# Softmax maximum over the keys: one GpSimd all-reduce in place of transposes, a row maximum and a copy

## The chip, the cores and the metric

The kernel runs on one core of a Trainium2 chip. Its engines are TensorE (PE, with its weight loads PEld), VectorE (DVE), ScalarE (ACT), GpSimd (POOL) and SyncE (SP), each with its own queue of instructions, worked off in order. The metric is the device time of one execution in microseconds, lower is better.

## The reference

One layer of a bidirectional encoder in float32: 2048 tokens of width 1024 with 16 learned meta tokens ahead of them (2064 keys). Four query heads share two key/value heads of width 128, beside them runs a Fourier mixing group, then an output projection and an MLP of width 4096. The part that matters here is the softmax over all keys:

```
s = jnp.einsum('bkgqd,bksd->bkgqs', qb, kt).astype(jnp.float32) * scale
p = jax.nn.softmax(s, axis=-1).astype(vt.dtype)
return jnp.einsum('bkgqs,bksd->bkgqd', p, vt)
```

For each query and head the maximum over all 2064 keys is subtracted ahead of the exponential.

## The kernel before

The program runs in stages: projections of the tokens (to about 310 us), attention (softmaxes from 346 to 985 us), and the MLP with its products in the Strassen manner (to the end). Attention shares its time with other work that is traced between its steps: the Fourier group's transforms, the output projection of the Fourier part (`out_f`, tiles pof, ysq, rs_f, xo) and that of the attention part (`out_a` and `flip`, tiles poa, rs_a, rs_m, h, pmt).

Attention has 16 units, each with 256 queries of two heads (512 columns) against all keys. A unit has 17 steps, one for each block of 128 keys and a last one for the meta tokens (`K = NT + 1`). Scores lie with the keys on the partitions and the 512 query columns in the free dimension:

- `scores(u, i)`: three products give a block of scores in PSUM, ScalarE copies it into an S tile (L780, two blocks to a tile), VectorE keeps the running maximum M over the blocks (L783 for the first, L786, L788, and L775 for the meta tokens). M is one tile with one buffer (`bufs=1`); at the end M[partition, column] is the maximum over the keys that share a partition.
- `stats(u)`: takes M over the 128 partitions and spreads the result to all of them, as the tile mb. `over_keys` (L794, L796) makes four TensorE transposes of 128x128 into the PSUM tile pm_m and a VectorE row maximum mx_m (128x4). `rows_to_cols` (L803) makes four more transposes of broadcast columns into pd_m, and ScalarE copies pd_m to mb (L811).
- `softmax(u, i)`: VectorE subtracts mb from an S tile (L840; L820 for the meta tokens), ScalarE takes the exponential (L841), VectorE sums (L845, L847), TensorE multiplies with V (L849, tile o).
- `finish(u)`: the sums over the keys go through `over_keys` and `rows_to_cols` as well (tiles pm_l, mx_l, pd_l), and the result is scaled and stored.

The PSUM tiles pm_m, pd_m, pm_l, pd_l and pys share one bank ("misc"). The scores run ahead of the softmax by one unit and three steps (`more(n + 1 + K + LEADT)`, LEADT = 3). `stats` of a unit is a generator: its first part is traced a step after that unit's last scores, its second part one step later, and `softmax(u, 0)` follows. The S tiles have 11 buffers, so the scores can't run further ahead.

GpSimd has three kinds of work in attention: the loads of K, q and V from DRAM (L704, L738, L713), the adds of squares ysq (L954) and the powers of -0.5 that give the norms' factors rs_f, rs_a and rs_m (L192, in `rstd_of`, a `tensor_tensor` with `ALU.pow`).

The order of the instructions on each engine is set at build time by the framework's scheduler, from the traced order, priorities and its own costs of the instructions; on the chip each engine then keeps that order and waits on semaphores.

Of the kernel before, what the change touches and what calls it, by code (L numbers as in the profile page):

```python
# [5 lines left out]

# [5 lines left out]
F32 = mybir.dt.float32  # L12
R32 = mybir.dt.float32r
AF = mybir.ActivationFunctionType
ALU = mybir.AluOpType
# [4 lines left out]
P = 128  # L20
# [68 lines left out]
def bc(ap, shape):  # L89
    return ap.broadcast_to(shape)  # L90
# [45 lines left out]
def encoder_block(ctx: ExitStack, tc: tile.TileContext, x, meta, w_in, w_f,  # L136
                  w_out, w_up, w_down, g_fin, g_cols, g_rows, c_id, c_rope, c_dft, c_even, c_odd, c_rem, out):
    nc = tc.nc
# [553 lines left out]
    ap2 = Lines(tc.alloc_tile_pool(name="ap2", bufs=1, side="right", reuse_waits="tile"), small)  # L692

    def misc(name, shape=(P, 512)):
        return app.tile(list(shape), F32, name=name, tag="misc")
# [33 lines left out]
    def attention():  # L729
# [60 lines left out]
        def over_keys(x, name, op):  # L790

            ps = misc("pm_" + name, (P, 4, P))
            for a in range(4):
                nc.tensor.transpose(ps[:, a], x[:, a * P:(a + 1) * P], ident)  # L794
            r = ap2.tile([P, 4], F32, name="mx_" + name, tag="mx", bufs=2)
            nc.vector.tensor_reduce(r, ps, axis=AX.X, op=op)  # L796
            return r

        def rows_to_cols(vec, name):

            ps = misc("pd_" + name, (P, 4, P))
            for a in range(4):
                nc.tensor.transpose(ps[:, a], bc(vec[:, a:a + 1], [P, P]), ident)  # L803
            return ps.rearrange("p a e -> p (a e)")

        def stats(u):
            s = state[u]
            r = over_keys(s["M"], f"m{u}", ALU.max)
            yield
            mb = s["mb"] = ap2.tile([P, 512], F32, name=f"mb_{u}", tag="mb", bufs=2)  # L810
            nc.scalar.copy(mb, rows_to_cols(r, f"m{u}"))  # L811

        def softmax(u, i):

# [76 lines left out]
        def more(upto):  # L891
            while ahead[0] < min(upto, total):
                w, i = divmod(ahead[0], K)
                if i == K // 2 and w < len(units) - 1:
                    start(w + 1)
                scores(w, i)
                loads_next("k", w, i)
                ahead[0] += 1
                if i == NT:
                    later.append(stats(w))  # L900
# [6 lines left out]
        for n in range(total):  # L907
            u, i = divmod(n, K)
# [826 lines left out]
```

## Time and profile before

| what | value |
|---|---|
| median of 3 runs | 2256.49 us (2255.51 to 2256.86) |
| the profiled execution | 2255.64 us, its span 2253.6 us |
| granted TensorE clock | 0.999 |
| busy: PE, DVE, ACT, POOL | 99%, 75%, 52%, 11% of the span |
| maxima over the keys | 16, the first begun at 343.6 us, the last at 956.1 us |

A row of a group reads: line, engine, operation, output<-inputs, shapes, count, then the busy time and the mean of one in ns, then the idle time of the engine ahead of them and what ended it. In a timeline a row begins with the start and the duration in us. "x2" merges two instructions that follow each other. PE's durations overlap, since matmuls are pipelined: the distance between two starts is the price of one.

### The profile page before, as it was taken

Reading aid. Unit: us, or ns where it says so; the run is one execution under the profiler, and the core shown is the slowest. Engines: PE = TensorE matmul, PEld = TensorE weight load, DVE = VectorE, ACT = ScalarE, POOL = GpSimd, SP = SyncE. Lnnn points to the kernel's source line nnn. Section 1 sums busy time; section 2 is a strip of 40 time slices with the busy share of each in tenths; the row PEclk is TensorE's granted clock in tenths of the full one; section 3 lists DMA queues with packets and bytes.
Section 4 is the critical chain, followed back from the end, with each engine's and each line's share of the span. In section 5 each row is a group of like instructions: output and inputs, shape, how many; then the busy total and the mean of one; then the engine's idle time right before and its main releaser. Section 6 shows DMA issues by size and latency. Waiting matters only on the chain.

```text
span 2253.6 us, 28116 instructions
## 1 busy us (share of the span) xinstructions
PE 2233.3 (99%) x10238; PEld 1771.3 (79%) x10238; DVE 1692.9 (75%) x2250; ACT 1178.1 (52%) x1997; POOL 247.8 (11%) x285
## 2 busy tenths in 40 slices
PE   9999999999999999999999999999999999999998
PEld 7898987766667666677888888888888888888887
DVE  6334579999999889788677668788765656796795
ACT  6443356666555566668556563334455545443343
POOL 2212120003322122110000020000110000200000
PEclk9999999999999999999999999999999999999999
DMA  6332253123344434357777576445594444954342
GB/s 205 90 108 70 86 149 90 52 65 130 113 133 131 158 128 133 137 208 256 264 233 241 181 290 227 132 143 167 185 362 169 154 154 152 343 178 159 126 137 84
DMA packets 191786, 367.40 MB, mean 163 GB/s; under 512 B 15760, under 2 KB 74768, under 8 KB 189984
## 3 DMA queue, kind: packets, MB, share of 16 engines
q1 hardware_dynamic: 171040, 310.08, 40.8%
q0 software_dynamic: 20464, 55.27, 7.6%
q8 instruction: 80, 1.31, 0.2%
q14 instruction: 58, 0.48, 0.1%
q10 hardware_dynamic: 144, 0.26, 0.0%
HBM read 236.28 MB, written 129.27 MB: 162 GB/s over the span
## 4 chain that ended last, share of the span: by engine, by line
PE 89%; DVE 5%; ACT 2%; DMA 1%; issue 1%; POOL 1%; SPq 0%; POOLq 0%; ACTq 0%; DVEq 0%
PE o L849 7%; PE ux L82 5%; PE ux L80 5%; PE ux L81 5%; PE dx L82 5%; PE dx L81 5%; PE dx L80 5%; PE dy L82 4%; PE dy L81 4%; PE dy L80 4%; PE uy L82 4%; PE uy L80 4%; PE uy L81 4%; PE s L80 2%; PE s L82 2%; PE s L81 2%
## 5 line engine op out<-in xcount | busy, mean ns | idle before, releaser
L70 ACT CAST ah<-a 128x1024 fp32r<-128x1024 f32 x108 | 113.0, 1050 | 263.2 <-PE dx L81 108.5
L849 PE MATMUL o<-S,vn 128*128 128x512 f32 x512 | 243.6, 596 | 4.2 <-ACT S L841 3.4
L780 ACT COPY S<-s 128x512 f32<-128x512 f32 x256 | 145.0, 584 | 92.4 <-PE s L82 73.1
L82 PE MATMUL dx<-bh,al 128*128 128x512 f32 x496 | 192.5, 388 | 0.0
L81 PE MATMUL dx<-bl,ah 128*128 128x512 f32 x496 | 192.5, 388 | 0.0
L80 PE MATMUL dx<-bh,ah 128*128 128x512 f32 x496 | 192.5, 388 | 0.0
L82 PE MATMUL ux<-bf,wul 128*128 128x512 f32 x448 | 174.2, 389 | 0.7 <-DVE wul L71 0.7
L80 PE MATMUL ux<-bf,wuh 128*128 128x512 f32 x448 | 174.6, 390 | 0.0
L81 PE MATMUL ux<-bf,wuh 128*128 128x512 f32 x448 | 174.3, 389 | 0.0
L840 DVE TENSOR_TENSOR S<-S,mb 128x1024 f32<-128x1024 f32 x128 | 155.1, 1227 | 11.7 <-ACT mb L811 11.6
L841 ACT ACTIVATE S<-S 128x1024 f32<-128x1024 f32 x128 | 135.1, 1062 | 43.0 <-DVE S L840 41.8
L71 DVE TENSOR_TENSOR al<-a,ah 128x1024 fp32r<-128x1024 f32 x108 | 131.2, 1219 | 31.6 <-ACT ah L70 31.3
L849 PEld LDWEIGHTS o<-S,vn 128*128 128x128 f32 x512 | 92.1, 189 | 75.2 <-issue 59.0
L80 PE MATMUL dy<-bh,ah 128*128 128x512 f32 (+1 forms) x388 | 150.5, 388 | 0.0
L81 PE MATMUL dy<-bl,ah 128*128 128x512 f32 (+1 forms) x388 | 150.5, 388 | 0.0
L82 PE MATMUL dy<-bh,al 128*128 128x512 f32 (+1 forms) x388 | 150.5, 388 | 0.0
L80 PE MATMUL s<-q,kt 128*128 128x512 f32 (+1 forms) x272 | 145.3, 534 | 2.3 <-ACT S L780 2.0
L80 PE MATMUL uy<-bf,wuh 128*128 128x512 f32 x320 | 125.0, 391 | 0.3 <-ACT wuh L70 0.3
L82 PE MATMUL uy<-bf,wul 128*128 128x512 f32 x320 | 124.6, 390 | 0.7 <-DVE wul L71 0.7
L81 PE MATMUL uy<-bf,wuh 128*128 128x512 f32 x320 | 124.8, 390 | 0.0
L786 DVE TENSOR_TENSOR M<-M,S 128x1024 f32<-128x1024 f32 x96 | 117.6, 1225 | 8.9 <-ACT S L780 8.0
L1212 ACT ACTIVATE c<-c 128x512 f32<-128x512 f32 x96 | 60.5, 631 | 119.4 <-DVE c L1260 116.6
(323 smaller groups left out, 5708.3 us busy)
## 6 DMA issues: line engine op xcount, KB each, us to landing
a<-s_d SPq DMA_DIRECT2D x84, 512.0 KB, 3.7
R<-in_w_up_dram SPq DMA_DIRECT2D x32, 1024.0 KB, 5.5
s_d<-s SPq DMA_DIRECT2D x128, 256.0 KB, 2.1
s_d<-c SPq DMA_DIRECT2D x96, 256.0 KB, 2.7
d<-in_w_down_dram SPq DMA_DIRECT2D x48, 512.0 KB, 5.2
f_d<-lf SPq DMA_DIRECT2D x56, 256.0 KB, 2.8
bf<-f_d SPq DMA_DIRECT2D x7, 2048.0 KB, 14.3
a<-s_d POOLq DMA_DIRECT2D x24, 512.0 KB, 7.3
```

Of the source, the lines that this page charges most:

```text
L70: self.high = nc.scalar.copy(hi, src)
L71: self.low = nc.vector.tensor_tensor(lo, src, f32v(hi), op=ALU.subtract)
L80: nc.tensor.matmul(out, a[0], b[0], start=first, stop=False, skip_group_check=chain)
L81: nc.tensor.matmul(out, a[0], b[1], start=False, stop=False, skip_group_check=chain)
L82: nc.tensor.matmul(out, a[1], b[0], start=False, stop=last, skip_group_check=chain)
L780: nc.scalar.copy(S[:, i % 2], ps)
L786: nc.vector.tensor_tensor(M, M, S, op=ALU.max)
L840: nc.vector.tensor_tensor(S, S, mb, op=ALU.subtract)
L841: nc.scalar.activation(p, S, AF.Exp, scale=ISQ)
L849: nc.tensor.matmul(s["O"], v[:, 2 * j % 4 + e], p[:, e], start=i + e == 1, stop=False)
L1212: nc.scalar.activation(dst, src, AF.Relu)
```

## The change

`partition_all_reduce` is one GpSimd instruction that reads M (128x512), takes the maximum over the 128 partitions and writes it to all partitions of mb. It stands in place of `over_keys`, `rows_to_cols` and the copy in `stats`. The rest of attention is as it was, the sums' transposes too. The generator still has one yield, now behind the whole work, so mb is complete in its first part.

```diff
+from concourse import bass_isa
...
         def stats(u):
             s = state[u]
-            r = over_keys(s["M"], f"m{u}", ALU.max)
-            yield
             mb = s["mb"] = ap2.tile([P, 512], F32, name=f"mb_{u}", tag="mb", bufs=2)
-            nc.scalar.copy(mb, rows_to_cols(r, f"m{u}"))
+            nc.gpsimd.partition_all_reduce(mb, s["M"], P, bass_isa.ReduceOp.max)
+            yield
```

More of the change, by code (lines that the diff above doesn't have):

```diff
@@ L807, in stats @@
             s = state[u]
-            r = over_keys(s["M"], f"m{u}", ALU.max)
+            mb = s["mb"] = ap2.tile([P, 512], F32, name=f"mb_{u}", tag="mb", bufs=2)
+            nc.gpsimd.partition_all_reduce(mb, s["M"], P, bass_isa.ReduceOp.max)
             yield
-            mb = s["mb"] = ap2.tile([P, 512], F32, name=f"mb_{u}", tag="mb", bufs=2)
-            nc.scalar.copy(mb, rows_to_cols(r, f"m{u}"))
         def softmax(u, i):
```

## The prediction

> **What bounds the kernel now.** I read the page first (busy shares, slices), then the busy times by stage, the groups of instructions, the waits, and last the timelines around one maximum. All rows are of the profile of before.
>
> ```profile
> span 2253.6 us, 28116 instructions
> ...
> PE 2233.3 (99%) x10238; PEld 1771.3 (79%) x10238; DVE 1692.9 (75%) x2250; ACT 1178.1 (52%) x1997; POOL 247.8 (11%) x285
> ```
>
> The shares over the whole span say: TensorE is the bound, GpSimd has nothing to do. But the edit lives in attention alone, between the first maximum (343 us) and the last softmax (985 us), and there the balance is another one. Columns of the next view: stretch, its length, then busy time of each engine.
>
> ```profile
> 343.00:420.00 77.00, 76.63 (x358) 53.79 (x357) 74.26 (x90) 48.77 (x78) 6.49 (x10) 1.00 0.27 74
> 420.00:660.00 240.00, 235.81 (x987) 160.03 (x986) 232.01 (x290) 145.95 (x250) 53.07 (x47) 1.00 0.31 99
> 660.00:985.00 325.00, 322.58 (x1279) 219.95 (x1278) 286.83 (x356) 197.95 (x323) 63.31 (x53) 1.00 0.39 131
> ```
>
> VectorE is idle for 77 - 74.26 = 2.7 us in the first stretch, 8.0 us in the second and 38.2 us in the third. So for the first 317 us two engines, TensorE and VectorE, are both full; only after 660 is VectorE loose. GpSimd is busy 20% of the time. Granted TensorE clock is 1.00 throughout.
>
> **What is removed.** The edit drops these four groups (16 units, each with 4 + 4 transposes, a row maximum and a copy):
>
> ```profile
> L794 PE MATMUL pm_m<-ident,M 128*128 128x128 f32 x64 | 9.9, 277 | 1.0 <-DVE M L775 1.0
> L803 PE MATMUL pd_m<-ident,mx_m 128*128 128x128 f32 x64 | 10.1, 278 | 0.2 <-DVE mx_m L796 0.2
> L796 DVE TENSOR_REDUCE mx_m<-pm_m 128x4 f32<-128x512 f32 x16 | 11.0, 689 | 6.1 <-PE pm_m L794 5.8
> L811 ACT COPY mb<-pd_m 128x512 f32<-128x512 f32 x16 | 9.4, 585 | 16.5 <-PE pd_m L803 16.4
> ```
>
> Matmuls overlap, so TensorE's price is the distance between starts, not the 277 ns:
>
> ```profile
> 656.83 0.60 PE L794 MATMUL pm_m<-ident,M 128*128 128x128 f32 x4
> 657.26 1.02 PE L849 MATMUL o<-S,vn 128*128 128x512 f32 x2
> 658.21 0.65 PE L803 MATMUL pd_m<-ident,mx_m 128*128 128x128 f32 x4
> 658.61 0.48 PE L80 MATMUL s<-q,kt 128*128 128x512 f32 x1
> ```
>
> 657.26 - 656.83 = 0.43 and 658.61 - 658.21 = 0.40: 0.83 us a unit, 16 x 0.83 = 13.3 us of TensorE. VectorE loses 16 x 0.69 = 11.0 us of work, ScalarE 9.4 us (half idle, worth nothing by itself). The one-bank "misc" PSUM tile is also free sooner for the sums' transposes; that removes waits of tenths of a microsecond at most, counted as nothing. The 128 transposes of the sums stay.
>
> **What is added: one all-reduce of 128x512 on GpSimd per unit.** No row shows it. The nearest are GpSimd's two-input adds:
>
> ```profile
> 543.01 0.72 POOL L954 TENSOR_TENSOR ysq<-ysq 128x256 f32<-128x256 f32 x1 [19.60 <-ACT ysq L952]
> 545.23 0.45 POOL L954 TENSOR_TENSOR ysq<-ysq 128x128 f32<-128x128 f32 x1
> 702.68 1.25 POOL L954 TENSOR_TENSOR ysq<-ysq 128x256 f32<-128x256 f32 x2
> ```
>
> From 128 to 256 elements 0.27 us more: 2.1 ns an element and 0.18 us to start; one pass over 512 elements is 1.26 us. That is the floor: the data must at least go once through the engine. The other end is a reduction that takes lanes one by one; with 16 passes it is 0.18 + 16 x 1.08 = 17.5 us. I take four passes (read and fold within a group of partitions, carry across the groups, carry back, write to all partitions): 0.18 + 4 x 1.08 = 4.5 us, an estimate nearer to the floor, because every row of this engine here is a streaming pass.
>
> The Trainium skill (GPSIMD Engine Reference, Cross-partition — where GPSIMD wins) has a reduction along the partitions of [128, 2048] at 247,699 ns, which by a quarter would be an estimate of 61.9 us for our 512; no run so far shows this instruction. By it the sum would gain 16 x (61.9 - 0.7) - 48.9 = 930 us.
>
> **What it does to VectorE.** While GpSimd reads SBUF, VectorE's operations with two SBUF inputs stand still, and the other way round:
>
> ```profile
> 545.95 2.16 DVE L840 TENSOR_TENSOR S<-S,mb 128x1024 f32<-128x1024 f32 x1
> 548.03 1.48 DVE L786 TENSOR_TENSOR M<-M,S 128x1024 f32<-128x1024 f32 x1
> ...
> 546.26 2.16 POOL L954 TENSOR_TENSOR ysq<-ysq 128x256 f32<-128x256 f32 x2
> ...
> L840 DVE TENSOR_TENSOR S<-S,mb 128x1024 f32<-128x1024 f32 x128 | 155.1, 1227 | 11.7 <-ACT mb L811 11.6
> L786 DVE TENSOR_TENSOR M<-M,S 128x1024 f32<-128x1024 f32 x96 | 117.6, 1225 | 8.9 <-ACT S L780 8.0
> ```
>
> These two took (2.16 - 1.23) + (1.48 - 1.23) = 1.18 us longer than their means while GpSimd did 1.25 us of adds (its unhindered time, above). VectorE pays GpSimd's reading nearly one for one. The reverse:
>
> ```profile
> 894.56 6.61 POOL L192 TENSOR_TENSOR rs_m<-ms_m,mhalf 128x1 f32<-128x1 f32 x1 [7.14 <-DVE ms_m L190]
> ...
> 895.52 1.22 DVE L786 TENSOR_TENSOR M<-M,S 128x1024 f32<-128x1024 f32 x1
> ...
> 900.67 0.74 DVE L1057 SCALAR_TENSOR_TENSOR h<-poa,rs_a,h 128x512 f32<-128x512 f32 x1
> ...
> L192 POOL TENSOR_TENSOR rs_m<-ms_m,mhalf x16: 545/1458/6612, 805.7 to 1025.1; 128x1 f32<-128x1 f32 x16
> ```
>
> A power of one column, 0.55 us at its best, took 6.61 us: it came through when VectorE reached an operation fed from PSUM. So the all-reduce first waits for a break in VectorE's chain (this costs no VectorE time, but makes mb late), then holds VectorE for its 4.5 us. Behind the wait stand, on VectorE, the subtraction L840, and L783 of the next unit, since M has one buffer, which is now held until the all-reduce has read it; on GpSimd's queue the K, q and V loads, the squares' adds and the powers.
>
> **The sum by stretch.** Each unit takes from VectorE 4.5 - 0.69 = 3.81 us net. The maxima are 3, 6 and 7 in the three stretches:
>
> ```profile
> L796 DVE TENSOR_REDUCE mx_m<-pm_m x3: 690/691/692, 344.3 to 414.2; 128x4 f32<-128x512 f32 x3
> ...
> L796 DVE TENSOR_REDUCE mx_m<-pm_m 128x4 f32<-128x512 f32 x6 | 4.1, 686 | 0.8 <-PE pm_m L794 0.7
> ...
> L796 DVE TENSOR_REDUCE mx_m<-pm_m 128x4 f32<-128x512 f32 x7 | 4.8, 692 | 4.6 <-PE pm_m L794 4.5
> L840 DVE TENSOR_TENSOR S<-S,mb 128x1024 f32<-128x1024 f32 x64 | 76.6, 1220 | 10.2 <-ACT mb L811 10.2
> ```
>
> First stretch: 3 x 3.81 - 2.7 idle = +8.7 us. Second: 6 x 3.81 - 8.0 = +14.9. In both VectorE becomes the bound and TensorE's savings there are not collected. Third: 7 x 3.81 = 26.7 us fit into 38.2 idle, of which 10.2 + 4.5 = 14.7 us are waits for this very maximum, which the all-reduce replaces; TensorE is the bound and would save 7 x 0.83 = 5.8, of which I credit half, -2.9, since mb comes later. Together +20.7 us. What is late next there is rs_m and rs_a behind the all-reduce.
>
> **The queue of GpSimd.** All-reduces now alternate with tensor_tensor work of another kind, and the engine may have to fetch other code each time:
>
> ```profile
> L954 POOL TENSOR_TENSOR ysq<-ysq x32: 453/960/6802, 503.2 to 736.5; 128x256 f32<-128x256 f32 x16, 128x128 f32<-128x128 f32 x16
> ...
> L796 DVE TENSOR_REDUCE mx_m<-pm_m x11: 676/691/692, 530.2 to 956.4; 128x4 f32<-128x512 f32 x11
> ...
> L192 POOL TENSOR_TENSOR rs_m<-ms_m,mhalf 128x1 f32<-128x1 f32 x10 | 23.9, 2391 | 94.0 <-DVE ms_m L190 94.0
> L192 POOL TENSOR_TENSOR rs_f<-ms_f,mhalf 128x1 f32<-128x1 f32 x16 | 11.3, 707 | 70.6 <-DVE ms_f L190 64.8 <-PE s L82 5.8
> ...
> L713 POOL DMA_DIRECT2D vn<-v_n x20 | 11.5, 579 | 86.4 <-PE o L849 63.2 <-PE pa L567 17.4 <-PE pof L81 5.8
> ...
> vn<-v_n POOLq DMA_DIRECT2D x20, 256.0 KB, 3.1
> ...
> L1069 ACT ACTIVATE h<-h,rs_m 128x1024 f32<-128x1024 f32 x10 | 11.5, 1151 | 16.7 <-POOL rs_m L192 15.5 <-DMA h_d<-h 1.3
> ```
>
> No row shows such a fetch. Bounds: nothing (code resident), or two in each of the 11 units after 503, each at the price of a V load, 0.58 + 3.1 = 3.7 us: 81 us. Some 58 of those tensor_tensors (32 + 16 + 10) fall into 985 - 503 = 482 us, one per 8.3 us, so a fetch of 3.7 us is met by one in 3.7 / 8.3 = 45% of cases: 11 x 0.45 x 3.7 = 18 us, else GpSimd's idle time hides it. ScalarE already waits 15.5 us for rs_m, the rest has slack; I take half, +10 us. If that cover were gone it would be up to the 81.
>
> The Trainium skill (GPSIMD Engine Reference, Instruction dispatch) gives some 6 us for the first call to freshly loaded GpSimd code. By that price this term would be an estimate of 16 us instead of 10, and no row here shows it.
>
> **Total.** 20.7 + 10 = +30.7 on the profiled execution's own 2255.64 us (span 2253.6): 2286.3. That execution lies 0.85 us under the median of the runs, 2256.49; in terms of the median I predict 2287.
>
> **Rivals.**
> 1. *All hidden, faster.* If the all-reduce streams in one pass (1.26 us), it takes 0.57 us net from VectorE, 1.7, 3.4 and 4.0 us in the stretches, all inside the idle time, and the chain from M to the first subtraction is shorter than now:
>
> ```profile
> 342.90 0.69 DVE L775 TENSOR_TENSOR M<-M,S 96x512 f32<-96x512 f32 x1
> ...
> 346.39 1.23 DVE L840 TENSOR_TENSOR S<-S,mb 128x1024 f32<-128x1024 f32 x1 [1.36 <-ACT mb L811]
> ```
>
> 346.39 - 343.59 = 2.8 us today. Then TensorE collects its 13.3: 2256.5 - 13.3 = 2243. It turns at the price where the second stretch has no idle left: 0.69 + 8.0 / 6 = 2.0 us per all-reduce. For it: nothing on the chain is then longer. Against it: a cross-partition result needs more than one pass.
>
> 2. *Lane-serial, far slower.* At 17.5 us VectorE loses 16 x 16.8 - 48.9 = 220 us: with the 10 about 2486. For it: the engine's rows here show no crossing of partitions at all. Against it: a streaming design is what they do show. The Trainium skill's figure above belongs to this case, as its far end.
>
> 3. *Code fetches on the path.* The 4.5 us hold and every fetch is paid: 2256.5 + 20.7 + 81 = 2358. For it: mb, rs_a and rs_m are each awaited. Against it: GpSimd is idle 80% of the time and a fetch needs no data.
>
> 4. *No change.* An all-reduce of about 2 us and some gain on TensorE cancel: 2252 to 2261.
>
> **Chances.** Forecast 0.53 (2262 to 2347; the top is an all-reduce of eight passes, 8.8 us: 16 x 8.1 - 48.9 + 10 = +91), rival 1 0.18, rival 4 0.09, rival 2 0.12, rival 3 0.08. 0.2% is 4.5 us, about what a measurement of this kernel can tell from no change. Faster 0.18, same 0.09, slower 0.73. The range 2243 to 2347 leaves out rival 2, most of rival 3 and a little below rival 1.
>
> **What would show it.** The all-reduce's own row (4.5 us when VectorE is idle, more where it waits for a break); VectorE's L840 and L783 waiting for POOL mb, not ACT mb; two-input VectorE rows above 1.23 us around it; TensorE's idle time in the first two stretches grown by some 31 us (23.6 longer, 9 x 0.83 less work), led by S of L841; rs_m and rs_f later. From 985 us on every stage should keep its length. I am wrong if the all-reduce's row is under 2 us or over 9 us, if VectorE runs on undisturbed beside it, or if the build-time order of the engines puts enough other VectorE work behind each maximum.

## The result, and the profile after

| kernel | median | runs | ratio to before, 95% interval |
|---|---|---|---|
| before | 2256.68 us | 4 | |
| after | 2274.41 us | 4 | 1.0083 [1.0061, 1.0105] |

The change costs 17.7 us (14 to 24 by the interval). The profiled execution took 2274.24 us, with a span of 2272.4 us.

The page of the kernel after, its span and busy times:

```profile
span 2272.4 us, 27939 instructions
...
PE 2233.3 (98%) x10110; PEld 1761.9 (78%) x10110; DVE 1684.1 (74%) x2234; ACT 1173.1 (52%) x1981; POOL 271.1 (12%) x301
```

No engine works longer but GpSimd, and that by 23 us. So the 17.7 us are no added work: the engines wait. (TensorE's busy time has stayed the same with 128 products fewer; a part of that is a lower clock, to which the last section comes back.) The busy times by stage, same stretches as before:

```profile
343.00:420.00 77.00, 74.24 (x324) 49.31 (x322) 69.37 (x82) 45.90 (x73) 14.73 (x13) 1.00 0.25 70
420.00:660.00 240.00, 229.26 (x913) 152.48 (x914) 223.09 (x276) 139.43 (x236) 62.51 (x48) 0.98 0.29 95
660.00:985.00 325.00, 312.17 (x1200) 211.08 (x1198) 272.71 (x340) 189.52 (x310) 68.15 (x64) 0.99 0.40 131
```

TensorE idles 2.8 + 10.7 + 12.8 = 26.3 us of these 642, where it idled 7.0 before. VectorE, which I expected to become the bound, idles more too: 7.6, 16.9 and 52.3 us against 2.7, 8.0 and 38.2. Nothing is full any more; the engines wait for each other.

The stretches are fixed and the work in them slides, so the place of the loss is read from landmarks. The last step of each maximum, with its number and its first and last start: first the rows of before up to the sixth maximum, the ninth and the last, with the first `ux` product of the MLP; then the same rows of after (there the first maximum began just ahead of the window, hence x5 and x8).

```profile
L775 DVE TENSOR_TENSOR M<-M,S x6: 678/686/689, 342.9 to 528.4; 96x512 f32<-96x512 f32 x6
L775 DVE TENSOR_TENSOR M<-M,S x9: 676/685/689, 342.9 to 653.1; 96x512 f32<-96x512 f32 x9
L775 DVE TENSOR_TENSOR M<-M,S x16: 676/686/689, 342.9 to 955.0; 96x512 f32<-96x512 f32 x16
L80 PE MATMUL ux<-bf,wuh x448: 389/389/504, 1034.8 to 1941.4; 128*128 128x512 f32 x150
```

```profile
L776 DVE TENSOR_TENSOR M<-M,S x5: 678/681/683, 375.6 to 530.2; 96x512 f32<-96x512 f32 x5
L776 DVE TENSOR_TENSOR M<-M,S x8: 674/681/941, 375.6 to 664.8; 96x512 f32<-96x512 f32 x8
L776 DVE TENSOR_TENSOR M<-M,S x16: 674/681/941, 342.1 to 973.0; 96x512 f32<-96x512 f32 x16
L81 PE MATMUL ux<-bf,wuh x448: 389/389/497, 1053.6 to 1960.2; 128*128 128x512 f32 x150
```

Up to the sixth maximum after is 1.8 us late (530.2 against 528.4), at the ninth 11.7, at the sixteenth 18.0; the MLP starts 18.8 us later and keeps its length. The first maximum had come 0.8 us earlier than in before, so 2.6 us are lost up to the sixth. Most of the loss begins at about 530 us, when the output projection's adds and powers come onto GpSimd's queue (the first such add of before starts at 503.2). TensorE's products with S in before, between 343 and 985 us, and then the groups of after that answer to those shown of before:

```profile
L849 PE MATMUL o<-S,vn 128*128 128x512 f32 x511 | 243.2, 596 | 4.2 <-ACT S L841 3.4 <-ACT O L855 0.7
```

```profile
L810 POOL PARTITION_ALL_REDUCE mb<-M x16: 1800/1802/4948, 346.8 to 979.1; - x16
...
L840 DVE TENSOR_TENSOR S<-S,mb 128x1024 f32<-128x1024 f32 x128 | 156.9, 1237 | 27.6 <-POOL mb L810 27.6
L849 PE MATMUL o<-S,vn 128*128 128x512 f32 x512 | 248.3, 607 | 12.8 <-ACT S L841 11.3
L810 POOL PARTITION_ALL_REDUCE mb<-M x16 | 35.9, 2242 | 93.4 <-issue 39.5 <-DVE M L776 11.8 <-DVE wol L75 7.9
```

The all-reduce takes 1.80 us, not 4.5. VectorE's subtraction waits 27.6 us for it, where it waited 11.6 for ScalarE's mb, and TensorE waits 11.3 us for the S behind that, where it waited 3.4. And GpSimd itself idles 39.5 us ahead of its all-reduces on "issue", which means: for nothing that the profile shows. One such place, the seventh maximum. GpSimd's timeline:

```profile
573.48 0.56 POOL L193 TENSOR_TENSOR rs_f<-ms_f,mhalf 128x1 f32<-128x1 f32 x1
...
574.58 0.73 POOL L739 DMA_DIRECT2D q<-q_d  x1
582.47 1.80 POOL L810 PARTITION_ALL_REDUCE mb<-M  x1 [7.16 <-issue]
591.57 1.53 POOL L193 TENSOR_TENSOR rs_f<-ms_f,mhalf 128x1 f32<-128x1 f32 x1 [7.30 <-DVE mx_l L797]
```

VectorE's and TensorE's at the same time:

```profile
572.18 0.67 DVE L776 TENSOR_TENSOR M<-M,S 96x512 f32<-96x512 f32 x1
...
584.30 1.23 DVE L840 TENSOR_TENSOR S<-S,mb 128x1024 f32<-128x1024 f32 x1 [5.89 <-POOL mb L810]
585.56 0.68 DVE L825 TENSOR_TENSOR ph<-S,ph 32x512 fp32r<-32x512 f32 x1
...
586.30 0.79 PE L829 MATMUL o<-ph,vm 96*128 96x512 f32 x1 [5.82 <-DVE ph L825]
```

M is complete at 572.85. GpSimd has nothing left to do from 575.31 and still starts only at 582.47; mb comes at 584.27, 11.4 us after M. VectorE stands at L840, and behind it in VectorE's queue stands `ph` of the unit before, for which TensorE waits 5.8 us. Such a gap of 5.8 to 7.9 us stands ahead of 12 of the 16 all-reduces, all those with a `tensor_tensor` as the last computing instruction ahead of them on GpSimd. The other four (the second to the fifth maximum) follow another all-reduce and start 0.1 to 0.2 us after M. A gap of some 7 us stands on the way back, too (584.27 to 591.57). This is what a fetch of other code looks like here: idle time with no named cause, on each change of kind. That the time goes into fetching code is inferred from this pattern; no row names it.

### The profile page after: what moved, and what is told of

Read it like the earlier page. It is cut to its first block, busy times and chain, and to the rows that moved or that the text cites. A ratio compares the mean times of both kernels' runs of the same rounds, so it can differ in the third digit from the quotient of the medians.

```text
span 2272.4 us, 27939 instructions
## 1 busy us (share of the span) xinstructions
PE 2233.3 (98%) x10110; PEld 1761.9 (78%) x10110; DVE 1684.1 (74%) x2234; ACT 1173.1 (52%) x1981; POOL 271.1 (12%) x301
## 4 chain that ended last, share of the span: by engine, by line
PE 87%; DVE 7%; issue 2%; POOL 2%; ACT 1%; DMA 1%; SPq 0%; POOLq 0%; DVEq 0%; ACTq 0%
PE o L849 7%; PE ux L83 5%; PE ux L81 5%; PE ux L82 5%; PE dx L83 5%; PE dx L82 5%; PE dx L81 5%; PE dy L82 4%; PE dy L83 4%; PE dy L81 4%; PE uy L81 4%; PE uy L82 4%; PE uy L83 4%; PE s L81 2%; PE s L83 2%
## 5 line engine op out<-in xcount | busy, mean ns | idle before, releaser
L849 PE MATMUL o<-S,vn 128*128 128x512 f32 x512 | 248.3, 607 | 12.8 <-ACT S L841 11.3
L840 DVE TENSOR_TENSOR S<-S,mb 128x1024 f32<-128x1024 f32 x128 | 156.9, 1237 | 27.6 <-POOL mb L810 27.6
L841 ACT ACTIVATE S<-S 128x1024 f32<-128x1024 f32 x128 | 135.0, 1061 | 76.2 <-DVE S L840 75.8
```

What stands on the lines that cost most here:

```text
L840: nc.vector.tensor_tensor(S, S, mb, op=ALU.subtract)
L841: nc.scalar.activation(p, S, AF.Exp, scale=ISQ)
L849: nc.tensor.matmul(s["O"], v[:, 2 * j % 4 + e], p[:, e], start=i + e == 1, stop=False)
```

## The experiments

The theory after this reading: the hold of VectorE is small, and the 17.7 us come from fetching code on GpSimd at each change between `tensor_tensor` and the all-reduce. The rival: the hold of VectorE by the all-reduce is the cost, the gaps are hidden. A third possibility is the order of the instructions, which the build sets anew for every kernel; the traces show which kernels share it. In what follows a difference is one of medians, each taken against the kernel before in its own job, and the figure behind a time is its ratio to before, with the 95% interval.

**Without `tensor_tensor` on GpSimd in attention.** Both kernels get the same edit: the powers by logarithm and exponential on ScalarE, the squares' adds on VectorE. The first run is the kernel after, the second the kernel before.

```diff
+    nc.scalar.preload_act_table_set("natural_log_exp_and_others")
...
-        nc.gpsimd.tensor_tensor(rs[:rows], ms[:rows], mhalf[:rows, :n], op=ALU.pow)
+        if tag in ("f", "a", "m", "m2"):
+            nc.scalar.activation(rs[:rows], ms[:rows], AF.Ln)
+            nc.scalar.activation(rs[:rows], rs[:rows], AF.Exp, scale=-0.5)
+        else:
+            nc.gpsimd.tensor_tensor(rs[:rows], ms[:rows], mhalf[:rows, :n], op=ALU.pow)
...
-                nc.gpsimd.tensor_tensor(sq[:, :n], sq[:, :n], sq[:, n:2 * n], op=ALU.add)
+                nc.vector.tensor_tensor(sq[:, :n], sq[:, :n], sq[:, n:2 * n], op=ALU.add)
```

> The changed kernel with the all-reduce as the only code of its kind on GpSimd during attention: the powers rs_f, rs_a, rs_m become two ScalarE instructions (logarithm, exponential of -0.5 times it), the adds of ysq go to VectorE. Theory A (GpSimd fetches other code before each all-reduce that follows tensor_tensor work and again after it, some 6 us each, and mb waits for it): the gaps of 5.8 to 7.9 us ahead of the all-reduces from the sixth unit on and the gaps of 7 us behind them go, M to mb is 2 to 4 us in all 16 units, and the kernel is 15 to 30 us faster than the changed one, at or below the kernel before (2240 to 2260). Theory B (the all-reduce holds VectorE: 16 x 1.8 - 11.0 = 18 us): the hold stays, 2268 to 2280. Theory C (the loss lies in the order that the build set): no telling, but near 2274.

> Control: the kernel before with the same move of powers and adds off GpSimd, the transposes kept. All theories: within 6 us of the kernel before (2250 to 2260), since VectorE does the adds in 0.7 us a tile pair where GpSimd held it for 1.2. Theory A: e1 lies 0 to 13 us under this one (TensorE's 13.3 us less work, minus what mb comes later). Theory B: e1 lies about 18 us above it.

Measured: 2253.63 us, 0.9988 [0.9979, 0.9998], for the all-reduce; 2251.10 us, 0.9976 [0.9966, 0.9986], for the transposes. The edit is worth 5.8 us in the kernel before, and 17.7 + 3.3 = 21.0 us in the kernel after. So 15.2 us of the change's 17.7 are there only while `tensor_tensor` and all-reduces alternate; the intervals of the three kernels leave some 6 us either way on that. Without the alternation the all-reduce stands 2.5 us behind the transposes, where the fetch theory had expected it 0 to 13 us ahead of them and the rival 18 us behind. So the rival doesn't carry the result. The gaps ahead of the all-reduces are gone, as the fetch theory says: from the second maximum on each starts 0.1 to 0.2 us after M. The edit also changed the order on the engines (some 400 of VectorE's 2234 instructions of after stand elsewhere), so that a part of the 15.2 us comes from the order is not excluded by this pair. GpSimd's timeline around the first maximum shows the one fetch that is left, since the stages ahead of attention still use `tensor_tensor`:

```profile
340.52 0.72 POOL L744 DMA_DIRECT2D q<-q_d  x1 [7.92 <-PE s L83]
347.87 1.80 POOL L815 PARTITION_ALL_REDUCE mb<-M  x1 [6.63 <-issue]
```

**The first fetch, ahead of time.** The all-reduce kernel of the last pair, with an all-reduce of one column of the first scores into a tile that nobody reads, so that the code is there before the first maximum.

```diff
+            if u == 0 and i == 1:
+                first = ap2.tile([P, 1], F32, name="first", tag="first", bufs=1)
+                nc.gpsimd.partition_all_reduce(first, S[:, 0, :1], P, bass_isa.ReduceOp.max)
```

> e1 with one more all-reduce, of one column of the first score tile into a tile that nobody reads, on GpSimd at about 331 us: so that the fetch of the all-reduce's code is done before the first maximum is complete. In e1 the first maximum was 6.1 us from M to mb where it is 2.8 with transposes, and e1's units stood 2 to 3 us behind those of e2 from then on. Fetch theory: the first M to mb falls to 2 to 2.5 us and the time by 2.5 to 4 us against e1, to 2249 to 2252, level with e2 (2251.1). If the 2.5 us between e1 and e2 come from the hold of VectorE instead: no change, 2253 to 2255.

Measured: 2249.24 us, 0.9963 [0.9951, 0.9976]: 4.5 us better than without it (the intervals leave some 3.5 us either way), faster than before and after. In the two traces M of the second maximum is complete at 374.34 instead of 377.19 us, that of the third at 410.41 instead of 415.10; the order on the engines differs in places here too. GpSimd's timeline:

```profile
331.21 0.59 POOL L716 DMA_DIRECT2D vm<-v_m  x1
339.44 0.94 POOL L789 PARTITION_ALL_REDUCE first<-S  x1 [7.64 <-ACT S L786]
340.26 0.90 POOL L744 DMA_DIRECT2D q<-q_d  x1
343.57 1.80 POOL L818 PARTITION_ALL_REDUCE mb<-M  x1 [2.41 <-DVE M L781]
```

The fetch now lies in the 7.64 us behind the V loads, where GpSimd is idle anyway, and mb is there 1.9 us after M. Against the transposes under the same conditions (-5.8 us) this is -7.8: 2.0 us better, less than the two intervals can tell apart. All fetches gone, the exchange of eight transposes, a reduction and a copy for the all-reduce is worth nothing that these runs can tell from zero.

**The price of the hold.** The same kernel with each all-reduce done twice, the second into a tile that nobody reads.

```diff
+            two = ap2.tile([P, 512], F32, name=f"two_{u}", tag="two", bufs=1)
+            nc.gpsimd.partition_all_reduce(two, s["M"], P, bass_isa.ReduceOp.max)
```

> e5 with every all-reduce of 128x512 done twice, the second into a tile that nobody reads: 16 more holds of 1.8 us (28.8 us), without any further code fetch. Hold theory: VectorE pays them in the stretches where it is full (the first 9 units, 16 us) and has room for a part of the rest: +12 to +28 us against e5, 2262 to 2279. If the hold costs nothing because VectorE runs on beside it or has the time: under +5 us.

Measured: 2264.79 us, 1.0034 [1.0021, 1.0046], 15.5 us over the kernel with one. The group of the second all-reduces, from GpSimd's groups between 343 and 985 us of this kernel:

```profile
L820 POOL PARTITION_ALL_REDUCE two<-M x16 | 36.7, 2296 | 0.0
```

At 1.80 us each, 28.8 us of the 36.7 are work, the rest is waiting inside the instruction. TensorE, VectorE and ScalarE have the same order as in the kernel with one, instruction for instruction, so the second all-reduce alone makes the difference. 15.5 / 28.8 = 0.54: a microsecond of it costs about half a microsecond of the kernel (the intervals leave some 4 us on the 15.5). It isn't on the way to mb: M to mb takes 1.9 us in most units, as with one. It lies over VectorE's first subtractions, and their group shows that, with one all-reduce and with two:

```profile
L848 DVE TENSOR_TENSOR S<-S,mb 128x1024 f32<-128x1024 f32 x128 | 153.8, 1216 | 14.5 <-POOL mb L818 14.4
L850 DVE TENSOR_TENSOR S<-S,mb 128x1024 f32<-128x1024 f32 x128 | 163.0, 1287 | 15.7 <-POOL mb L818 15.7
```

So 9.1 us of the hold are seen in this group; where the rest of the 15.5 us arises is not shown. This price can't be put on the first all-reduce: during the second ones VectorE is idle for 1.3 us of their 36.7, during the first ones for 14.8 us of 38.3, since it waits for them. What a first one costs by its hold stays open.

**Fetches off the path of the maximum, on the transposes.** The kernel before, with an all-reduce of one column of M into a tile that nobody reads.

```diff
+            junk = ap2.tile([P, 1], F32, name=f"jk_{u}", tag="jkm", bufs=2)
+            nc.gpsimd.partition_all_reduce(junk, s["M"][:, :1], P, bass_isa.ReduceOp.max)
```

> The kernel before with an added all-reduce of one column of M (128x1) into a tile that nobody reads, at the place of the changed kernel's; transposes, copy and mb as before. So there is the change of code on GpSimd, without the hold of 512 columns and without mb behind it. Theory A in its narrow form (only mb's wait costs): 0 to +4 us (2255 to 2261). Theory A in its wide form (the rs_f, rs_a, rs_m and ysq behind the fetch cost too): +5 to +12 us. Theory B: under +3 us. The row of the one-column all-reduce also gives its fixed price: 0.2 to 0.6 us, where 512 columns took 1.80.

Measured: 2264.05 us, 1.0033 [1.0021, 1.0045], +7.1 us. The instruction's own row (min/median/max):

```profile
L810 POOL PARTITION_ALL_REDUCE jk<-M x16: 345/738/1341, 347.8 to 967.0; - x16
```

Sixteen instructions of 0.35 to 1.34 us, whose result nobody awaits, cost 7.1 us, with TensorE's order nearly that of before (10232 of its 10238 instructions stand in the same sequence). mb doesn't stand behind the fetches here, but the powers and adds do: between 343 and 985 us VectorE's waits for rs_f and rs_a grow from 1.8 to 7.7 us, ScalarE's for rs_m from 15.5 to 16.5. That M is held longer costs VectorE 0.7 us. The shortest of them also prices the all-reduce: (1.80 - 0.35) / 511 = 2.8 ns a column over a fixed 0.35 us.

**The same number of fetches, on the path and off it.** Both start from the fastest kernel. The first puts a `tensor_tensor` of one column behind each all-reduce, so that the next all-reduce needs a fetch. The second adds a one-column all-reduce right behind that, so that the code is back before the next maximum is complete. `tiny` and `back` are read by nothing else.

```diff
+            tiny = ap2.tile([P, 1], F32, name=f"tiny_{u}", tag="tiny", bufs=2)
+            nc.gpsimd.tensor_tensor(tiny, mb[:, :1], mhalf[:, :1], op=ALU.mult)
```

```diff
+            back = ap2.tile([P, 1], F32, name=f"back_{u}", tag="back", bufs=2)
+            nc.gpsimd.partition_all_reduce(back, tiny, P, bass_isa.ReduceOp.max)
```

> e5 with one tensor_tensor of one column (a copy of mb's first column times a constant, unread) on GpSimd right behind each all-reduce: it makes GpSimd fetch the tensor_tensor code after each maximum and the all-reduce's code ahead of the next, and nothing but mb waits for either. As the q load stands between, waiting for the unit's last scores, the fetch ahead of the all-reduce begins only then. Fetch theory: M to mb rises from 2 us to 6 to 9 us in nearly all 16 units, and the time by 10 to 35 us against e5, to 2259 to 2284. If the fetch is harmless and only the powers and adds behind it cost in the changed kernel: under +4 us, 2249 to 2253.

> e9 with an all-reduce of one column, unread, right behind the one-column tensor_tensor: as many fetches, one there and one back in each unit, but both done while GpSimd has nothing else to do, so that the all-reduce's code lies ready when M is complete. Fetch theory (the price is the wait of mb, not the fetch itself): M to mb stays at 2 to 2.5 us in nearly all units, the time within 4 us of e5, 2248 to 2254. If the fetches themselves slow the other engines (their traffic, or a held port): near e9.

Measured: 2255.52 us, 0.9996 [0.9987, 1.0005], with the fetch on the path, 6.2 us over the kernel without; 2250.89 us, 0.9974 [0.9964, 0.9984], with it off the path, 1.5 us over, inside the intervals. GpSimd around the thirteenth maximum, first on the path (and the fifteenth maximum of the same run), then off it:

```profile
825.34 0.90 POOL L744 DMA_DIRECT2D q<-q_d  x1 [22.25 <-PE s L83]
833.45 1.80 POOL L818 PARTITION_ALL_REDUCE mb<-M  x1 [7.21 <-DVE ms_m L192]
...
909.64 1.80 POOL L818 PARTITION_ALL_REDUCE mb<-M  x1 [8.29 <-DVE M L781]
```

```profile
820.05 0.90 POOL L744 DMA_DIRECT2D q<-q_d  x1 [17.24 <-PE s L83]
821.04 1.80 POOL L818 PARTITION_ALL_REDUCE mb<-M  x1
829.86 0.18 POOL L820 TENSOR_TENSOR tiny<-mb,mhalf 128x1 f32<-128x1 f32 x1 [7.02 <-issue]
...
837.69 4.28 POOL L822 PARTITION_ALL_REDUCE back<-tiny  x1 [6.79 <-issue]
```

On the path, M is complete at 826.49 and the all-reduce starts 7 us later; the `ms_m` that its row names is only the last event ahead of it, it is no input of it. GpSimd had been idle 22.25 us up to the q load, for which it waits on the unit's last scores, and only behind that load the fetch begins: that is why it falls between M and mb in 13 of the 16 units, though the engine has time enough. The last two maxima have no q load ahead of them; there the gap is over before M is complete, and the all-reduce starts 0.1 us after M (at 909.64, M at 909.50). In the second kernel both fetches (7.02 and 6.79 us) run after mb is delivered, and cost next to nothing; TensorE, VectorE and ScalarE have the same order there as in the fastest kernel, instruction for instruction. So a fetch isn't dear by its length but by what stands behind it.

On the path the order is not quite that of the fastest kernel (9800 of TensorE's 10110 instructions stand in the same sequence), so a part of the 6.2 us can be the order. But TensorE's waits for the exponentials of S and for `ph`, both behind the subtraction, grow from 1.5 to 7.9 us between 343 and 985 us, about as much as was lost. The sign was as expected; the size (6.2 us for 13 delayed maxima, 0.5 us each) lies under the 10 us that I had expected at least. M to mb adds up to 101 us in this kernel and to 103 us in the kernel after (38 us in the fastest), so the delay of mb is probably only one part of the 15.2, and the powers' and adds' delay another. The two, 6.2 and 7.1 us, come to 13.3 of 15.2, from kernels that aren't quite the same.

**Three edits that lost.** The q load on SyncE's queue, in the kernel after, to let the fetch begin earlier:

```diff
-            nc.gpsimd.dma_start(q, q_d[b][:, :, 2 * g:2 * g + 2])
+            nc.sync.dma_start(f32v(q), q_d[b][:, :, 2 * g:2 * g + 2])
```

> The changed kernel with the q loads issued by SyncE in place of GpSimd. In the changed kernel the q load waits on GpSimd's queue for the unit's last scores, and the code fetch can't begin before it, so that some 3 to 6 us of the fetch come after M is complete. Theory A: the fetch begins earlier, M to mb falls from a mean of 7 us towards 3 to 4 us in the later units where the q load stood ahead (8 of 11), and the time falls by 5 to 15 us (2260 to 2269). Theory B: no change, 2272 to 2277.

Measured: 2295.75 us, 1.0168 [1.0153, 1.0184], 21 us slower than after, where a gain of 5 to 15 us or no change was expected. The first maximum is late already (M is complete at 348.7 us, in after at 342.8); TensorE's scores waited once for a q, 3.2 us, and VectorE waits 7.8 us for rs_a, where it waited 2.8 in after. The rows of the tile q and of VectorE's groups between 343 and 985 us:

```profile
  DMA q<-q_d: 3.2, 1
...
L1057 DVE SCALAR_TENSOR_TENSOR h<-poa,rs_a,h 128x512 f32<-128x512 f32 x17 | 12.7, 747 | 13.8 <-POOL rs_a L193 7.8 <-PE poa L83 6.0
```

The order on the engines changed with it, and in several units the K load or an add of squares took q's place as the last thing ahead of the fetch. So the time says nothing for or against the theory, and where most of the 21 us come from is not worked out. The starts of the all-reduces do fit it: ahead of the ninth maximum GpSimd's last instruction, an add, ended at 654.80 us, 13 us before M (667.84), and the all-reduce started at 667.98; ahead of the eighth the last one, an add too, ended 0.9 us before M, and the all-reduce started 5.0 us after M.

The sum over the groups of squares by four accumulating products on TensorE instead of two adds, first in the fastest kernel, then in the transposing one without `tensor_tensor`:

```diff
-            for n in (2, 1):
-                nc.vector.tensor_tensor(sq[:, :n], sq[:, :n], sq[:, n:2 * n], op=ALU.add)
...
-            nc.tensor.matmul(ps, ops[t].pop()[:, 0], ones, start=True, stop=True)
+            sq = ops[t].pop()
+            for k in range(NG):
+                nc.tensor.matmul(ps, sq[:, k], ones, start=k == 0, stop=k == NG - 1)
```

> e5 with the sum of the four groups of squares taken by four accumulating products with ones on TensorE, in place of VectorE's adds and one product. Theory: with the all-reduce VectorE is the bound of the stretches around 420 to 770 us and TensorE has some 10 us to spare there, so giving 11 us of VectorE work (16 x 0.69) to TensorE (48 more products of one column, some 0.17 us each, 8 us) brings 3 to 8 us: 2242 to 2248. If TensorE is the bound after all: 0 to +8 us, 2250 to 2258.

> Control for e6: e2 (transposes, nothing but loads on GpSimd) with the sum of squares on TensorE. TensorE was busy 653 of 657 us there, so its 8 us more count: +2 to +8 us against e2, 2253 to 2259. If VectorE bounds e2 as well: 0 to -4 us, 2247 to 2251.

Measured: 2260.30 us, 1.0013 [1.0005, 1.0022], and 2261.87 us, 1.0021 [1.0012, 1.0031]: 11.0 and 10.6 us worse than without, both above all that was expected. TensorE's timeline, with four products a tile, then with one (each product is two records):

```profile
543.91 0.94 PE L967 MATMUL pys<-ones,ysq 128*128 128x1 f32 x8
544.72 0.49 PE L81 MATMUL pof<-wfh,yh 128*128 128x512 f32 x1
```

```profile
541.53 0.28 PE L967 MATMUL pys<-ones,ysq 128*128 128x1 f32 x2
541.67 0.48 PE L83 MATMUL pof<-wfh,yl 128*128 128x512 f32 x1
```

From start to start 0.81 us instead of 0.14, and if all 16 are like this one, 10.7 us, about the whole loss. TensorE idles 10.3 and 3.8 us of the 642 in the two kernels from which these started; the work put on it was paid in full, and taking the adds from VectorE brought nothing.

## Why the prediction was right, and for which reasons

The direction and the size held: +30.7 predicted, +17.7 measured. The two terms behind them did not: one was far too large, the other too small, and that the two errors partly made up for each other was luck.

*The price of the all-reduce was mis-sized.* I took four passes, 4.5 us; it takes 1.80, near the floor of one pass, 1.26. This is below the 2 us at which I called myself wrong. The figure that the Trainium skill gives in GPSIMD Engine Reference, Cross-partition — where GPSIMD wins, for another instruction (an estimate of 61.9 us here) isn't borne out for this one by the 1.80 us.

*The term of +20.7 us* for VectorE's hold against TensorE's saving: the runs put it at -2.0, not told from zero. With 1.80 us my own balance gives rival 1, "all hidden, faster", whose turning point was 2.0. It did not come either; without the fetches the picture is that of rival 4, an all-reduce of about 2 us and TensorE's gain that cancel. My balance charged an all-reduce only when VectorE's idle time over a whole stretch was used up, and the doubling shows that this is too little. With 3, 6 and 7 more all-reduces of 1.80 us against the 3.15, 6.55 and 38.74 us in which VectorE idled there (77, 240 and 325 us less its busy times below), it gives 5.40 - 3.15 + 10.80 - 6.55 = 6.5 us, and 15.5 came out. The busy times of the fastest kernel in the three stretches:

```profile
343.00:420.00 77.00, 75.55 (x329) 51.30 (x328) 73.85 (x88) 49.33 (x77) 14.91 (x15) 1.00 0.30 81
420.00:660.00 240.00, 236.44 (x963) 159.96 (x961) 233.45 (x309) 147.95 (x265) 24.65 (x22) 0.99 0.31 100
660.00:985.00 325.00, 319.73 (x1254) 218.98 (x1253) 286.26 (x370) 203.56 (x366) 27.74 (x29) 1.00 0.42 140
```

Idle time summed over a stretch isn't idle time at the right place.

*The term of +10 us for fetches* was the true cost, and too small: 15.2 us for the later units and 4.5 us for the first maximum, 19.7 together. Three of its parts were off. The price of one is 5.8 to 7.9 us ahead of the all-reduce and about 7 us back, not 3.7. (The Trainium skill, GPSIMD Engine Reference, Instruction dispatch, gives some 6 us for a first call to freshly loaded code; the gaps here, 5.8 to 7.9 us, are about that.) The fetch ahead of the first maximum was left out, since I counted only the 11 units after 503. And the working charged 11 fetches, where its own bound of 81 us counts 22; with 22 it gives 22 x 0.45 x 3.7 / 2 = 18 us. (The estimate of 16 us beside it made the fetch longer, but not more often met: with 6 / 8.3 = 72% it would be 24.) The share that I took as paid, 10 of 81 us, was met by luck: 12 fetches before and 11 after at 7 us would be some 160 us, of which 19.7 were paid, 12% in both cases; but my working held only GpSimd's own `tensor_tensor` work against a fetch, and not the wait of mb. Rival 3, all of them on the path, is excluded by this. The reason against it, that a fetch needs no data, was wrong: it waits for its place in the queue, behind a q load that waits for the unit's last scores.

So -2.0 + 19.7 = 17.7, against 20.7 + 10 = 30.7: an error of -22.7 and one of +9.7. The three measured parts add up because they are differences of the same medians; that is no check of them. The total was nearer than its parts.

*Step by step.* VectorE's L840 waits for POOL mb, as foretold; L783 (now L784) doesn't wait for it, its row has no idle time of note. Two-input rows stretch hardly (L840 1.237 us in the mean against 1.227), since the all-reduce mostly runs while VectorE waits for it (VectorE is idle for 21.7 us of its 35.9); where VectorE is in a chain, the all-reduce gives way (4.95 us at the longest). TensorE's idle time grew by 19.3 us in the three stretches, not by 31 in the first two (there by 8.9), and the growth is led by S of L841 (from 3.4 to 11.3) and by `ph` (from nothing to 7.4), which stands behind L840. rs_m is hardly later: ScalarE waits 17.2 us for it instead of 15.5. But two of these waits now reach TensorE, since L841 stands behind them on ScalarE: 2.5 us up to 860.9 and 3.3 us up to 904.3. VectorE's waits for rs_f and rs_a grow from 1.8 to 6.0 us. From 985 us on the stages kept their length.

*Still open:* how the 15.2 us divide between the late mb, the late powers and adds, and a changed order of the instructions, and what the first all-reduce costs by its hold alone.

## What to carry to other kernels

Before an engine is given a new kind of instruction, count how often its kinds will alternate in its queue: on GpSimd each change between `tensor_tensor` and the all-reduce cost 6 to 8 us of an idle engine, and one small call of the coming kind, placed after the last urgent result, took these off the path. An engine that is 11% busy isn't free if its queue waits, for a load, exactly when it is wanted. And idle time summed over a stretch doesn't hide a hold of the bound's neighbour: doubling it prices an added one, though the copy may lie over other work than the first.

## What the runs showed of the hardware

TensorE's clock fell behind the new gaps. The busy times of three stretches of after (granted clock is the number behind the engines; before had 1.00 in all of attention):

```profile
540.00:550.00 10.00, 9.33 (x29) 5.65 (x30) 8.25 (x13) 5.24 (x11) 2.60 (x3) 0.83 0.16 54
...
580.00:590.00 10.00, 4.18 (x11) 2.67 (x10) 5.46 (x6) 2.62 (x5) 1.80 (x1) 0.66 0.15 55
...
900.00:910.00 10.00, 6.67 (x16) 3.82 (x15) 6.02 (x6) 5.81 (x9) 1.90 (x2) 0.68 0.29 105
```

TensorE's timeline behind the wait for `ph` shown above:

```profile
587.32 0.63 PE L82 MATMUL pof<-wfl,yh 128*128 128x512 f32 x1
587.74 0.63 PE L83 MATMUL pof<-wfh,yl 128*128 128x512 f32 x1
...
591.71 0.39 PE L81 MATMUL pof<-wfh,yh 128*128 128x512 f32 x1
591.93 0.39 PE L82 MATMUL pof<-wfl,yh 128*128 128x512 f32 x1
```

After 5.8 us of idleness the products follow each other at 0.42 us instead of 0.22, and the granted clock is back at 1.00 from 589.6: some 1.7 us lost on top of the 5.8. A second such place follows an idle time of 3.3 us (from 901 to 904.34), in which ScalarE had waited for rs_m, not for mb; there the clock is back at 910.5. The Trainium skill (TensorE: Matmul & The Clock Gate, Part 1: The HAM clock gate) gives half the rate after an idle window of about 3.4 us; these two places nearly agree with it, a third doesn't. Ahead of the half clock from 541.8 to 545.2 us no idle time is longer than 1.46 us (up to 539.33; one of 0.67 us follows), and 2.54 us of idleness up to 860.9 cost no clock (1.00 from 860 to 866). So the length of one gap doesn't tell here whether a stall costs more than its length.

The granted clock is at one half from 541.8 to 545.2, from 582.8 to 589.6 and from 903.6 to 910.5. TensorE was at work for 3.4 + 3.3 + 6.2 = 12.9 us of that, so half of it, about 6.4 us, is an estimate of what the clock cost within the 17.7. TensorE's busy time points the same way: 2233.3 us in after, and less in the run without `tensor_tensor` on GpSimd, with as many products:

```profile
PE 2223.7 (99%) x10110; PEld 1759.2 (78%) x10110; DVE 1687.4 (75%) x2266; ACT 1181.5 (52%) x2053; POOL 188.0 (8%) x233
```
